# Walking the moving columns of TensorE products in interleaved order, in one decoder block

## The chip, the cores and the metric

The kernel runs on one core of one Trainium2 chip. The metric is the device time of one execution in microseconds (us), the median over the runs shown. Beside it stands one profiled execution, whose trace gives every instruction's start and duration.

## The reference

One layer of a decoder block over 512 tokens of width 1024, in float32. What matters here:

```
proj = rmsnorm(x) @ w_in                     # split into q_r, k_r, v_r, g_r, q_s, k_s, v_s, gates
ret  = silu(g_r) * GroupNorm(retention(q_r, k_r, v_r))     # v_r, g_r: 512 x 1024
y_r  = ret @ w_ret_out;   y_s = sliding_window_attention(q_s, k_s, v_s) @ w_swa_out
x    = x + rmsnorm((sigmoid(gate_r) * y_r + sigmoid(gate_s) * y_s) @ w_out)
u    = square(relu(rmsnorm(x) @ w_up))       # 512 x 4096
x    = x + rmsnorm(u @ w_down)               # the down projection: 4096 -> 1024
```

## The kernel before

**Arithmetic.** Every large product is done in three passes of a rounded float32 type (fp32r): an operand is split into a rounded part and a remainder (`parts`, `split`, lines 135 and 136: a cast on ScalarE, ACT in the profile, and a subtraction on VectorE, DVE), and `mm3` (lines 179 to 181) issues three matmuls into the same accumulator. A matmul has a stationary operand of 128 x 128, which a weight load (PEld) brings in, and a moving operand whose columns stream through, 256 or 512 of them; result column c lands in column c of a bank of the accumulator memory (PSUM).

**Seven products in place of eight.** The large products are split 2 x 2 into blocks and formed by a Strassen-Winograd scheme. Two of these products have weights as the moving operand and are the ones in question.

*The retention's values and gates* (`wide`, for `w_v` and then `w_g`). The weights, in blocks of 512 columns that the host lays out (`wide_blocks`), or sums of blocks added in flight by DMA, are split (`moving_parts`) and streamed. Seven products of 2 token tiles x 4 contraction tiles x 3 passes are 168 matmuls of 512 columns for each of the two weights. The accumulators are tiles named `wide`; ScalarE and VectorE bring them into `vg`. `wide` is a generator: the caller steps it between other work, some 55 to 106 us after the start for the values and 164 to 207 us for the gates.

*The down projection* (554 us to the end). Seven products `p1` to `p7` run over the same 512 columns; the left operands are blocks of `uc` (`left`), the moving ones blocks of `w_down`, or sums that DMAs accumulate into `tch[j]` and `rb[j]` (`right`). Each runs over four chunks j, and in each over 2 x 2 contraction tiles, 2 token tiles and 3 passes: 24 matmuls for a chunk, 96 for a product (`product2`). One tile of `w_down` goes through several products. The steps stand in an order written out by hand: `p1`, `p2` and `p5` in turn; then for each j `p6`, `p3` and the `p7` of the chunk before; then `p4`. Of `p4`, 72 matmuls have 512 columns; the last 16 x 3 are done in halves of 256 columns, in tiles named `p4c`. The profile leaves digits out of names, so `p1` to `p7` are all called `p` there.

Blocks of weights come in by DMAs that SyncE (SP) and GpSimd (POOL) issue. Between these products stand the sliding-window attention, the gates and the up projection (`wino`, 256 columns), `pblk`, `yr`, `ys` and `ps`.

Of the kernel before, what the change touches and what calls it, by code (L numbers as in the profile page):

```python
# [16 lines left out]
P = 128  # L17
# [21 lines left out]
C_QR, C_KR, C_VR, C_GR, C_QS, C_KS, C_GATE_R = (0, 512, 1024, 2048, 3072, 3584, 3840)  # L39
# [42 lines left out]
    return np.ascontiguousarray(t)  # L82


def wide_blocks(w):

    return np.ascontiguousarray(w.reshape(2, 4, P, 2, 512).transpose(3, 0, 2, 1, 4))


def f(ap):  # L90
# [4 lines left out]
def block_kernel(ctx, tc, x, xT, pre_mix, w_in, w_v, w_g, w_gate, w_ret, w_swa, w_out, sinks, post_mix,  # L95
                 pre_mlp, w_up, w_down, post_mlp, decay, chunk, dist, out):
    nc = tc.nc
    x, out = x[0], out[0]
    w_in, w_ret, w_swa, w_out = (w[0] for w in (w_in, w_ret, w_swa, w_out))
# [31 lines left out]
    last = {}  # L131
# [467 lines left out]
    def wide_sums(pool, w_, **kw):  # L599

        both = pool.tile([P, 2, 4, 512], F32, name="acc", **kw)
        sx, sy = both[:, 0], both[:, 1]
        nc.sync.dma_start(sx, w_[1, 0])
        nc.gpsimd.dma_start(sx, w_[1, 1], accum_op=ALU.add)
        nc.sync.dma_start(sy, w_[0, 0])
        return sx, sy

    def wide(w_, sx, sy, out):

        def c(i, half, tb):  # L610
            return out[:, 2 * half + tb, i * 512 : (i + 1) * 512]

        def product(ps, w, y, first=True):
            for tb in range(2):
                for k in range(4):
                    mm3(
                        ps[tb], tuple(o[:, k, tb * P : (tb + 1) * P] for o in hB[y]), w[k],
                        first and k == 0, k == 3, not first,
                    )

        def two():
            return [bank([P, 512], "wide") for _ in range(2)]

        chain = two()
        w = moving_parts(sy)
        nc.gpsimd.dma_start(sy, w_[1, 0], accum_op=ALU.add)
        ws1 = moving_parts(sx)
        nc.gpsimd.dma_start(sx, w_[0, 0], accum_op=ALU.add)
        yield
        product(chain, w, "11")  # L630
        for tb in range(2):
            nc.scalar.copy(c(0, 0, tb), chain[tb])
        yield
        p5 = two()
        product(p5, ws1, "t1")
        for tb in range(2):
            last["copy"] = nc.scalar.copy(c(1, 1, tb), p5[tb])
        yield
        p2 = two()
        product(p2, moving_parts(wide_load(w_, 0, 1)), "21")  # L640
        for tb in range(2):
            nc.vector.tensor_tensor(c(0, 0, tb), p2[tb], c(0, 0, tb), op=ALU.add)
        yield
        with tc.issue_after(last["copy"].ins):
            w = moving_parts(sx)
        nc.gpsimd.dma_start(sx, w_[0, 1], accum_op=ALU.add)
        product(chain, w, "t2", False)
        for tb in range(2):
            nc.scalar.copy(c(0, 1, tb), chain[tb])
            nc.vector.tensor_tensor(c(0, 1, tb), c(0, 1, tb), c(1, 1, tb), op=ALU.add)  # L650
        yield
        product(chain, moving_parts(sy), "t3", False)
        for tb in range(2):
            after = nc.scalar.copy(c(1, 0, tb), chain[tb])
            nc.vector.scalar_tensor_tensor(
                c(1, 1, tb), c(1, 0, tb), -1.0, c(1, 1, tb), op0=ALU.mult, op1=ALU.subtract
            )
        yield
        product(chain, moving_parts(wide_load(w_, 1, 1)), "t4", False)
        for tb in range(2):  # L660
            nc.scalar.mul(c(1, 0, tb), chain[tb], -1.0)
        yield
        p3 = two()
        with tc.issue_after(after.ins):
            w = moving_parts(sx)
        product(p3, w, "22")
        for tb in range(2):
            nc.vector.tensor_tensor(c(0, 1, tb), p3[tb], c(0, 1, tb), op=ALU.add)
        yield
# [14 lines left out]
    for g in range(SWA_KV):  # L684
        ps = bank([P, SEQ])
# [5 lines left out]
    sv = wide_sums(accpool, w_v, tag="acc")  # L691
# [18 lines left out]
    def ret_query(w):  # L710
# [5 lines left out]
    qT, qc = ret_query(wqk[0])  # L716
    kT = ret_block(wqk[1])
    vg = vpool.tile([P, NT, D_MODEL], F32, name="vg", tag="vg")
    steps = wide(w_v, *sv, vg)
    next(steps)  # L720
    hB = wino_tokens(
        None, *(tuple(quad(a, i, j) for a in hT) for i in range(2) for j in range(2)),
        [quad(xTs, i, j) for i in range(2) for j in range(2)], hsum,
    )
# [15 lines left out]
    for h in range(RET_HEADS):  # L740
        if 0 < h < RET_HEADS - 1:
            wqk = load_qk(h + 1)
        v = parts(vg[:, :, h * RET_DV : (h + 1) * RET_DV], [P, NT, RET_DV])
        if h == RET_HEADS - 1:
            vg = vpool.tile([P, NT, D_MODEL], F32, name="vg", tag="vg")
            steps = wide(w_g, *wide_sums(xypool, w_g), vg)
            next(steps)
        kd = ret_keys(kT, h)
        pt = ret_scores(qT, kT, h)
        q_now = qc  # L750
        if h + 1 < RET_HEADS:
            qT = ret_block(wqk[0])
        else:
            next(steps)
        if h == 0:
            probs_t = swa_transpose(probs)
        states = ret_states(kd, v, h)
        if h == 0:
            swa_values(3, probs_t)

            bctx.close()
            gctx = ExitStack()
            wx = wino_pool(gctx)
            pad(wx, 64)
            xyctx = ExitStack()
            xypool = xyctx.enter_context(tc.tile_pool(name="xypool", bufs=1))
        if h + 1 < RET_HEADS:
            kT = ret_block(wqk[1])
        else:
            next(steps)  # L770
        ret_values(q_now, pt, states, v, h)
        if h + 1 < RET_HEADS:
            qc = [rpool.tile([P, SEQ - P], F32R, name=f"qc{i}", bufs=1) for i in range(2)]
            split(qc[0], qc[1], qT[:, P:])
# [117 lines left out]
    a = wino_first(gate_weights(0))  # L892
    for bp in range(KD // 2):
        a = gate(2 * bp, a, lambda: gate_weights(2 * bp + 1))
        wr = gate(2 * bp + 1, a, lambda: ret_weights(bp))
        if bp < KD // 2 - 1:
            a = wino_first(gate_weights(2 * bp + 2))
# [66 lines left out]
    for half in range(2):  # L964
        zs = [[None, None], [None, None]]
        for n in range(2):
            for t in range(2):
                tt = 2 * half + t
                ps = bank([P, 512])
# [6 lines left out]
        with tc.high_priority(offset=CHAIN_AHEAD):  # L976
            for t in range(2):
# [4 lines left out]
                for n in range(2):  # L982
                    c = slice(n * 512, (n + 1) * 512)
# [139 lines left out]
    a = wino_first(up_weights(NH))  # L1123
    for fp in range(NH, 16):
        a = up_pair(fp, a)
# [13 lines left out]
    def left(j, q):  # L1139
        hi, lo = (ring.tile([P, 4, 256], F32R, name=f"left{i}") for i in range(2))  # L1140
        split(hi, lo, uc[j][:, q])
        return hi, lo

    def right(src):
        return [parts(src[:, 2 * i : 2 * i + 2], [P, 2, 512]) for i in range(2)]

    def product(ps, a, b, h, first, last, tb, c=slice(0, 512)):
        for i in (2 * h, 2 * h + 1):
            mm3(
                ps[tb], tuple(o[:, i, tb * P : (tb + 1) * P] for o in a),  # L1150
                tuple(o[:, i % 2, c] for o in b[h]), first and i == 0, last and i == 3,
            )

    def product2(ps, j, a, b):
        for h in range(2):
            for tb in range(2):
                product(ps, a, b, h, j == 0, j == 3, tb)

    def t_add(dst, k, c, j):
        nc.gpsimd.dma_start(dst, w_down[k, c, j], accum_op=ALU.add)  # L1160
# [24 lines left out]
    def step_p2(j):  # L1185
        with tc.issue_after(last["chain2"].ins), tc.high_priority(offset=LEFT_AHEAD if j == 0 else 0):
            a, b = left(j, 2), right(load_b(1, 0, j, 4))
        product2(p2, j, a, b)

    def step_p5(j):  # L1190
        a, b = left(j, 1), right(tch[j])
        if j < T2_DMA:
            t_add(tch[j], 1, 1, j)

        nc.vector.tensor_tensor(uc[j][:, 1], uc[j][:, 1], uc[j][:, 0], op=ALU.add)
        nc.vector.tensor_tensor(uc[j][:, 0], uc[j][:, 3], uc[j][:, 1], op=ALU.subtract)
        product2(p5, j, a, b)

    for step, j in ((step_p1, 0), (step_p2, 0), (step_p1, 1), (step_p5, 0), (step_p2, 1),
                    (step_p1, 2), (step_p5, 1), (step_p2, 2), (step_p1, 3), (step_p5, 2),  # L1200
# [42 lines left out]
    p6, p3 = banks2("p6"), banks2("p3")  # L1243
    p7 = None
    rb = {}

    def step_p6(j):
        if j >= T2_DMA:
            nc.vector.tensor_tensor(tch[j], tch[j], rb[j], op=ALU.add)
        a, b = left(j, 1), right(tch[j])  # L1250
        t_add(tch[j], 1, 0, j)

        nc.vector.tensor_tensor(uc[j][:, 1], uc[j][:, 2], uc[j][:, 1], op=ALU.subtract)
        product2(p6, j, a, b)

    def step_p3(j):
        a, b = left(j, 1), right(rb[j])
        t_add(rb[j], 0, 1, j)
        product2(p3, j, a, b)

    def step_p7(j):
        product2(p7, j, left(j, 0), right(rb[j]))

    for j in range(4):
        rb[j] = load_b(1, 1, j)
# [22 lines left out]
    for j in range(2):  # L1288
        a, b = left(j, 3), right(tch[j])
        for h in range(2):  # L1290
            for tb in range(2):
                product(p4, a, b, h, j == 0, j == 1 and tb == 1, tb)
        combine(j)
    ab = [(left(j, 3), right(tch[j])) for j in (2, 3)]
    for tb in range(2):
# [4 lines left out]
            residual(tb, factor(tb), ((0, outz[tb]), (512, p1c[tb])))  # L1300
    for j in (2, 3):
        for h in range(2):
            product(p4, *ab[j - 2], h, False, j == 3, 0)
    nc.vector.tensor_tensor(u3[0], p4[0], u3[0], op=ALU.subtract)
    squares(2, 1, u3[0])
    weigh(0, u3[0])
# [59 lines left out]
```

## Time and profile before

| | |
|---|---|
| runs | 721.85 and 724.63 us, median 723.24 us |
| profiled execution | span of 719.9 us from the first to the last instruction; no time of its own outside the span is given for it |
| TensorE (PE) | 708.3 us busy, 4438 matmuls and as many weight loads |
| VectorE, ScalarE, GpSimd | 535.8, 421.7 and 60.3 us busy |
| granted TensorE clock | 0.999 |
| HBM | 114.96 MB read, 163 GB/s over the span |

In the rows of the profile, "128*128 128x512" after a matmul's names are the stationary shape and the moving operand's partitions and columns. A matmul's own duration (390 ns for 512 columns, on the page) overlaps with the next matmul; what a matmul costs in a stream is the distance from its start to the next one's, and it is read from the timeline.

### The profile page before, as it was taken

Reading aid. Unit: us, or ns where it says so; the run is one execution under the profiler, and the core shown is the slowest. Engines: PE = TensorE matmul, PEld = TensorE weight load, DVE = VectorE, ACT = ScalarE, POOL = GpSimd, SP = SyncE. Lnnn points to the kernel's source line nnn. Section 1 sums busy time; section 2 is a strip of 40 time slices with the busy share of each in tenths; the row PEclk is TensorE's granted clock in tenths of the full one; section 3 lists DMA queues with packets and bytes.
Section 4 is the critical chain, followed back from the end, with each engine's and each line's share of the span. In section 5 each row is a group of like instructions: output and inputs, shape, how many; then the busy total and the mean of one; then the engine's idle time right before and its main releaser. Section 6 shows DMA issues by size and latency. Waiting matters only on the chain.

```text
span 719.9 us, 11248 instructions
## 1 busy us (share of the span) xinstructions
PE 708.3 (98%) x4438; PEld 628.8 (87%) x4438; DVE 535.8 (74%) x808; ACT 421.7 (59%) x712; POOL 60.3 (8%) x75
## 2 busy tenths in 40 slices
PE   8999999999999999999999999999999999999996
PEld 7877878888888989989888999999999888888885
DVE  5699986667885667566845876877776788977797
ACT  6667676345665526344643776666668666655571
POOL 0200000201100000000002100000000110010010
PEclk9999999999999999999999999999999999999999
DMA  9964424916444455461563618777753999698603
GB/s 318 330 179 84 108 72 129 282 46 132 101 142 120 107 162 147 125 197 59 198 271 117 159 47 234 201 202 193 204 153 118 305 278 238 151 208 194 118 0 117
DMA packets 43605, 117.79 MB, mean 164 GB/s; under 512 B 3488, under 2 KB 21024, under 8 KB 37408
## 3 DMA queue, kind: packets, MB, share of 16 engines
q1 hardware_dynamic: 36784, 80.76, 31.8%
q0 software_dynamic: 6480, 36.18, 27.3%
q8 instruction: 35, 0.57, 0.3%
q14 instruction: 18, 0.15, 0.1%
q10 hardware_dynamic: 288, 0.14, 0.1%
HBM read 114.96 MB, written 2.10 MB: 163 GB/s over the span
## 4 chain that ended last, share of the span: by engine, by line
PE 79%; DVE 8%; DMA 5%; ACT 4%; issue 2%; POOL 0%; POOLq 0%; DVEq 0%; SPq 0%; ACTq 0%
PE wino L179 9%; PE wino L180 9%; PE wino L181 9%; PE p L181 5%; PE p L180 5%; PE p L179 5%; DVE wlo L136 3%; PE wide L179 3%; PE wide L180 3%; PE wide L181 3%; DMA raw<-in_w_in 3%; PE ps L180 2%; PE ps L181 2%; PE yr L181 2%; PE yr L180 2%; PE yr L179 2%
## 5 line engine op out<-in xcount | busy, mean ns | idle before, releaser
L136 DVE TENSOR_TENSOR wlo<-raw,whi 128x1024 fp32r<-128x1024 f32 x81 | 98.6, 1223 | 42.4 <-ACT whi L135 42.2
L135 ACT CAST whi<-raw 128x1024 fp32r<-128x1024 f32 x81 | 84.8, 1052 | 40.4 <-DMA raw<-in_w_down 7.6
L181 PE MATMUL p<-whi,left 128*128 128x512 f32 x216 | 84.1, 390 | 0.2 <-DVE left L136 0.2
L180 PE MATMUL p<-wlo,left 128*128 128x512 f32 x216 | 84.2, 390 | 0.0
L179 PE MATMUL p<-whi,left 128*128 128x512 f32 x216 | 84.0, 390 | 0.1
L181 PEld LDWEIGHTS p<-whi,left 128*128 128x128 f32 x216 | 40.5, 188 | 9.3 <-DVE left L136 1.0
L180 PEld LDWEIGHTS p<-wlo,left 128*128 128x128 f32 x216 | 40.5, 188 | 8.9 <-DVE wlo L136 0.4
L179 PEld LDWEIGHTS p<-whi,left 128*128 128x128 f32 x216 | 40.5, 188 | 8.7 <-ACT left L135 0.5
L136 DVE TENSOR_TENSOR wlo<-tch,whi 128x1024 fp32r<-128x1024 f32 x32 | 38.6, 1220 | 6.9 <-ACT whi L135 6.9
L135 ACT CAST left<-uc 128x1024 fp32r<-128x1024 f32 x28 | 29.3, 1050 | 23.4 <-PE p L180 23.4
L135 ACT CAST p<-rs 128x1024 fp32r<-128x1024 f32 x21 | 22.1, 1051 | 35.5 <-DVE rs L230 35.4
L136 DVE TENSOR_TENSOR left<-uc,left 128x1024 fp32r<-128x1024 f32 x28 | 34.1, 1221 | 10.4 <-ACT left L135 10.4
L135 ACT CAST whi<-tch 128x1024 fp32r<-128x1024 f32 x32 | 33.2, 1050 | 11.3 <-PE p L181 6.8
L136 DVE TENSOR_TENSOR p<-rs,p 128x1024 fp32r<-128x1024 f32 x21 | 25.7, 1226 | 15.4 <-ACT p L135 15.4
L136 DVE TENSOR_TENSOR wlo<-rs,whi 128x1024 fp32r<-128x1024 f32 x21 | 25.7, 1224 | 12.1 <-ACT whi L135 9.4
L136 DVE TENSOR_TENSOR wlo<-acc,whi 128x1024 fp32r<-128x1024 f32 x20 | 24.1, 1217 | 6.5 <-ACT whi L135 6.5
L179 PE MATMUL wino<-h2s,p 128*128 128x256 f32 x104 | 28.7, 276 | 0.0
L180 PE MATMUL wino<-h2s,p 128*128 128x256 f32 x104 | 28.7, 276 | 0.0
L181 PE MATMUL wino<-h2s,p 128*128 128x256 f32 x104 | 28.7, 276 | 0.0
L179 PE MATMUL wino<-h2c,whi 128*128 128x256 f32 x104 | 28.7, 276 | 0.0
L180 PE MATMUL wino<-h2c,whi 128*128 128x256 f32 x104 | 28.7, 276 | 0.0
L181 PE MATMUL wino<-h2c,wlo 128*128 128x256 f32 x104 | 28.7, 276 | 0.0
(354 smaller groups left out, 2317.7 us busy)
## 6 DMA issues: line engine op xcount, KB each, us to landing
tch<-in_w_down POOLq DMA_DIRECT2D x12, 1024.0 KB, 9.5
raw<-in_w_down SPq DMA_DIRECT2D x7, 1024.0 KB, 7.6
rs<-in_w_up SPq DMA_DIRECT2D x13, 512.0 KB, 4.2
rs<-in_w_up POOLq DMA_DIRECT2D x13, 512.0 KB, 5.7
raw<-in_w_up SPq DMA_DIRECT2D x13, 512.0 KB, 5.1
raw<-in_w_in SPq DMA_DIRECT2D x8, 512.0 KB, 5.2
acc<-in_w_v POOLq DMA_DIRECT2D x4, 1024.0 KB, 7.9
rs<-in_w_gate SPq DMA_DIRECT2D x8, 512.0 KB, 3.9
```

The costliest lines, as they stand in the source:

```text
L135: last["hi"] = nc.scalar.copy(hi, src)
L136: last["split"] = nc.vector.tensor_tensor(lo, src, f(hi), op=ALU.subtract)
L179: nc.tensor.matmul(ps, ah, bh, start=first, stop=False, skip_group_check=more)
L180: nc.tensor.matmul(ps, ah, bl, start=False, stop=False, skip_group_check=more)
L181: nc.tensor.matmul(ps, al, bh, start=False, stop=last, skip_group_check=more)
```

## The change

A pair (n, e) describes a walk. The 512 columns are seen as n blocks of equal size, and each block as runs of e columns. The walk takes the first run of every block, then the second run of every block, and so on. With (2, 4): columns 0 to 3, 256 to 259, 4 to 7, 260 to 263, ... Before, all columns are taken from 0 to 511.

| product | walk (n, e) | run, bytes | matmuls of 512 columns |
|---|---|---|---|
| values (`w_v`) | (2, 4) | 16 | 168 |
| gates (`w_g`) | (2, 16) | 64 | 168 |
| `p1` | none | | 96 |
| `p2` | (2, 4) | 16 | 96 |
| `p5` | (2, 16) | 64 | 96 |
| `p6` | (2, 2) | 8 | 96 |
| `p3` | (2, 32) | 128 | 96 |
| `p7` | (4, 8) | 32 | 96 |
| `p4` | (2, 64) | 256 | 72 |

In the down projection, the moving operand and the accumulator are both walked in this order, so every result column lands where it did. In `wide`, the host permutes the columns of each block of 512 beforehand; the walk undoes this, so the moving operand is read in the interleaved order while the accumulator is written from column 0 to 511. The halves of `p4c` keep the plain order. No instruction, DMA or wait is added or taken away in the source.

```
+ORDER_V, ORDER_G = (2, 4), (2, 16)
-def wide_blocks(w):
-    return np.ascontiguousarray(w.reshape(2, 4, P, 2, 512).transpose(3, 0, 2, 1, 4))
+def wide_blocks(w, order):
+    n, e = order
+    t = w.reshape(2, 4, P, 2, 512).transpose(3, 0, 2, 1, 4)
+    t = t.reshape(2, 2, P, 4, 512 // (n * e), n, e).transpose(0, 1, 2, 3, 5, 4, 6)
+    return np.ascontiguousarray(t.reshape(2, 2, P, 4, 512))
...
-    def wide(w_, sx, sy, out):
+    def wide(w_, sx, sy, out, order):
+        n, e = order
+        def streamed(ap):
+            return ap.rearrange("p (n q e) -> p q n e", n=n, e=e)
...
                     mm3(
-                        ps[tb], tuple(o[:, k, tb * P : (tb + 1) * P] for o in hB[y]), w[k],
+                        ps[tb].rearrange("p (q n e) -> p q n e", n=n, e=e),
+                        tuple(o[:, k, tb * P : (tb + 1) * P] for o in hB[y]),
+                        tuple(streamed(o) for o in w[k]),
                         first and k == 0, k == 3, not first,
                     )
...
-    def product(ps, a, b, h, first, last, tb, c=slice(0, 512)):
+    def streamed(ap, order):
+        if not order:
+            return ap
+        n, e = order
+        return ap.rearrange("p (n q e) -> p q n e", n=n, e=e)
+
+    def product(ps, a, b, h, first, last, tb, c=slice(0, 512), order=None):
         for i in (2 * h, 2 * h + 1):
             mm3(
-                ps[tb], tuple(o[:, i, tb * P : (tb + 1) * P] for o in a),
-                tuple(o[:, i % 2, c] for o in b[h]), first and i == 0, last and i == 3,
+                streamed(ps[tb], order), tuple(o[:, i, tb * P : (tb + 1) * P] for o in a),
+                tuple(streamed(o[:, i % 2, c], order) for o in b[h]), first and i == 0, last and i == 3,
             )
...
-        product2(p2, j, a, b)
+        product2(p2, j, a, b, (2, 4))
...
-        product2(p5, j, a, b)
+        product2(p5, j, a, b, (2, 16))
-        product2(p6, j, a, b)
+        product2(p6, j, a, b, (2, 2))
-        product2(p3, j, a, b)
+        product2(p3, j, a, b, (2, 32))
-        product2(p7, j, left(j, 0), right(rb[j]))
+        product2(p7, j, left(j, 0), right(rb[j]), (4, 8))
...
-                product(p4, a, b, h, j == 0, j == 1 and tb == 1, tb)
+                product(p4, a, b, h, j == 0, j == 1 and tb == 1, tb, order=(2, 64))
```

More of the change, by code (lines that the diff above doesn't have):

```diff
@@ L718, in block_kernel @@
     vg = vpool.tile([P, NT, D_MODEL], F32, name="vg", tag="vg")
-    steps = wide(w_v, *sv, vg)
+    steps = wide(w_v, *sv, vg, ORDER_V)
     next(steps)
@@ L745, in block_kernel @@
             vg = vpool.tile([P, NT, D_MODEL], F32, name="vg", tag="vg")
-            steps = wide(w_g, *wide_sums(xypool, w_g), vg)
+            steps = wide(w_g, *wide_sums(xypool, w_g), vg, ORDER_G)
             next(steps)
@@ L1145, in right, with product2 @@
         return [parts(src[:, 2 * i : 2 * i + 2], [P, 2, 512]) for i in range(2)]
-    def product(ps, a, b, h, first, last, tb, c=slice(0, 512)):
+    def streamed(ap, order):
[4 more added lines that the diff above has]
+    def product(ps, a, b, h, first, last, tb, c=slice(0, 512), order=None):
         for i in (2 * h, 2 * h + 1):
             mm3(
-                ps[tb], tuple(o[:, i, tb * P : (tb + 1) * P] for o in a),
-                tuple(o[:, i % 2, c] for o in b[h]), first and i == 0, last and i == 3,
+                streamed(ps[tb], order), tuple(o[:, i, tb * P : (tb + 1) * P] for o in a),
+                tuple(streamed(o[:, i % 2, c], order) for o in b[h]), first and i == 0, last and i == 3,
             )
-    def product2(ps, j, a, b):
+    def product2(ps, j, a, b, order=None):
         for h in range(2):
             for tb in range(2):
-                product(ps, a, b, h, j == 0, j == 3, tb)
+                product(ps, a, b, h, j == 0, j == 3, tb, order=order)
     def t_add(dst, k, c, j):
@@ L1302, in block_kernel @@
         for h in range(2):
-            product(p4, *ab[j - 2], h, False, j == 3, 0)
+            product(p4, *ab[j - 2], h, False, j == 3, 0, order=(2, 64))
     nc.vector.tensor_tensor(u3[0], p4[0], u3[0], op=ALU.subtract)
@@ L1348 @@
         pre_mix_norm=np.asarray(inputs["pre_mix_norm"]).reshape(KD, P).T,
-        w_v=wide_blocks(w_in[0, :, C_VR:C_GR]),
-        w_g=wide_blocks(w_in[0, :, C_GR:C_QS]),
+        w_v=wide_blocks(w_in[0, :, C_VR:C_GR], ORDER_V),
+        w_g=wide_blocks(w_in[0, :, C_GR:C_QS], ORDER_G),
         w_gate=pair_blocks(w_in[0, :, C_GATE_R:]),
```

## The prediction

> **What bounds the kernel now.** I read the page first, then the waits of TensorE, then the groups by shape, then the timeline for the distance between matmuls.
>
> ```profile
> span 719.9 us, 11248 instructions
> PE 708.3 (98%) x4438; PEld 628.8 (87%) x4438; DVE 535.8 (74%) x808; ACT 421.7 (59%) x712; POOL 60.3 (8%) x75
> PE 79%; DVE 8%; DMA 5%; ACT 4%; issue 2%; POOL 0%; POOLq 0%; DVEq 0%; SPq 0%; ACTq 0%
> ```
>
> TensorE is busy for 98% of the span, and 79% of the chain that ended last is its own work. The waits say the same; these are all that TensorE has:
>
> ```profile
> PE warm L336 <- POOL ident masks.py:199: 1.4, 1, 1.4
> PE ptok L179 <- ACT wkv L135: 1.3, 1, 1.3
> PE swa_s L430 <- ACT vg L637: 0.6, 1, 0.6
> PE pblk L181 <- DVE wlo L136: 0.5, 1, 0.5
> PE wino L179 <- ACT sgs L283: 0.2, 1, 0.2
> PE wide L179 <- ACT vg L654: 0.2, 1, 0.2
> PE tin L1040 <- ACT uc L1031: 0.2, 1, 0.2
> PE p L181 <- DVE left L136: 0.2, 1, 0.2
> ```
>
> They sum to 4.6 us in 720. So the time is the sum of the distances between matmuls, and a nanosecond on one of them reaches the end. The groups that the change touches, by count:
>
> ```profile
> L179 PE MATMUL p<-whi,left 128*128 128x512 f32 x216 | 84.0, 390 | 0.1
> L180 PE MATMUL p<-wlo,left 128*128 128x512 f32 x216 | 84.2, 390 | 0.0
> L181 PE MATMUL p<-whi,left 128*128 128x512 f32 x216 | 84.1, 390 | 0.2 <-DVE left L136 0.2
> L179 PE MATMUL wide<-whi,hsum 128*128 128x512 f32 x64 | 25.4, 397 | 0.2 <-ACT vg L654 0.2
> L179 PE MATMUL wide<-whi,hT 128*128 128x512 f32 x48 | 19.2, 399 | 0.0
> ```
>
> Three lines of 216 are the 648 matmuls of `p`; without the 96 of `p1`, which keeps its order, 552 change. `wide` has 64 + 48 on each of three lines, 336, and all change. Together 888 of 512 columns. Their 390 ns is passage, not cost; the cost is the distance between starts:
>
> ```profile
> 562.02 0.39 PE L179 MATMUL p<-whi,left 128*128 128x512 f32 x1
> ...
> 565.88 0.39 PE L181 MATMUL p<-whi,left 128*128 128x512 f32 x1
> 124.80 0.39 PE L180 MATMUL pblk<-hT,whi 128*128 128x512 f32 x1
> ...
> 127.37 0.40 PE L179 MATMUL pblk<-hT,whi 128*128 128x512 f32 x1
> 239.99 0.28 PE L179 MATMUL wino<-hsum,whi 128*128 128x256 f32 x1
> ...
> 242.48 0.28 PE L180 MATMUL wino<-hT,whi 128*128 128x256 f32 x1
> 269.93 0.28 PE L181 MATMUL wino<-hsum,wlo 128*128 128x256 f32 x1
> ...
> 271.93 0.28 PE L180 MATMUL wino<-hsum,p 128*128 128x256 f32 x1
> 392.94 1.91 PE L1040 MATMUL tin<-ident,zg 128*128 128x128 f32 x16
> ```
>
> From the first to the last of 18 `p` matmuls are 17 steps: 3.86 / 17 = 227.1 ns. Twelve of `pblk`, same shape, take 2.57 / 11 = 233.6 ns each. Of the 256-column ones, 23 take 2.49 / 22 = 113.2 ns and, 30 us later, 18 take 2.00 / 17 = 117.6 ns. Two things follow. Cost goes with the columns (227.1 is twice 113.2; 0.443 ns a column), with nothing left over for an instruction. And the same instruction on other tiles is up to 6.5 ns dearer (227.1 to 233.6), so how the columns are fetched does show.
>
> **The change part by part.** *What stays.* The counts of matmuls, weight loads, casts and DMAs are those of before, and no step is moved past another on any queue. The host's permutation of `w_v` and `w_g` leaves the blocks their shape, so their DMAs stay; sums and splits go element by element and do not care about column order. Accumulators end with the same columns in the same places, so what reads them stays. I cost all this at nothing, and no cover is needed for it.
>
> *What the walk costs on the 888 matmuls.* No row of this trace has a matmul that reads or writes in pieces, so I bound it by the nearest rows. Above: the slowest stream is that of the transposes (the x16 row above; one lasts 273 ns by the next row). (1.91 - 0.273) / 15 = 109 ns for 128 columns is 0.852 ns a column, about twice 0.443.
>
> ```profile
> L1040 PE MATMUL tin<-ident,zg 128*128 128x128 f32 x32 | 4.0, 273 | 0.2 <-ACT uc L1031 0.2
> L135 ACT CAST whi<-raw 128x1024 fp32r<-128x1024 f32 x81 | 84.8, 1052 | 40.4 <-DMA raw<-in_w_down 7.6
> L135 ACT CAST left<-uc 128x1024 fp32r<-128x1024 f32 x28 | 29.3, 1050 | 23.4 <-PE p L180 23.4
> ```
>
> A matmul of 512 columns at that rate costs 512 x 0.852 = 436 ns, 209 ns more than now; over 888 that would be 186 us. Below: if a column of a transpose takes two passes through the array, one pass is 0.426 ns at most, and a stream without loss would take 218 ns in place of 227.1: 9.0 ns saved on each, 8.0 us in all. Between these ends the nearest row is ScalarE's: 12 of the 81 casts from `raw` read eight runs of 128 columns out of 256 (lines that slice `raw[:, :, b * P : (b + 1) * P]`), and the group's mean is 1052 ns against 1050 for the plain reads of `left<-uc`. Twelve dearer ones in 81 can then hide 2 x 81 / 12 = 14 ns at most, under 2 ns a run. It is another engine and the runs are longer than any of the walk's, but it is the only row in which a walk in pieces is priced, and it prices it at next to nothing. So I take **nothing** for the walk, with both ends kept for the rivals.
>
> *Placement.* Within "nothing" the 6.5 ns between `p` and `pblk` stay open, as a walk also alters which part of memory is read at which moment: 888 x 6.5 ns = 5.8 us either way.
>
> *What is late next.* A slower stream gives the other engines more room. A faster one would run into them in the down projection:
>
> ```profile
> 554.00:631.00 77.00, 76.84 (x360) 63.81 (x358) 64.55 (x62) 48.66 (x56) 8.20 (x10) 1.00 0.89 239
> 631.00:704.00 73.00, 72.93 (x322) 60.12 (x321) 60.19 (x64) 43.00 (x49) 7.79 (x9) 1.00 0.61 126
> ```
>
> The columns are length, busy time of TensorE, weight loads, VectorE, ScalarE and GpSimd, clock, DMA share and GB/s. VectorE has 12 us spare in each stretch, so the 5 us that the down projection could gain would stay covered, except in the first stretch, where the DMA engines are at 0.89.
>
> *The sum.* The span is 719.9 us and the median of the runs shown 723.24, 3.3 us more, which I leave as lying around the span. 723.2 + 0 = **723.2 us**.
>
> *A page against it.* The trace has no row of a matmul that writes its accumulator in pieces. The Trainium skill, "PSUM — Partial Sum Buffer", section "Specifications (TRN2)", says that accumulator lines are 8 bytes and that any output that isn't contiguous slows matmuls significantly. By that, the 552 of `p` would be dear and the 336 of `wide`, written straight, would not; it is the third rival, priced there from rows. The Trainium skill, "SBUF — State Buffer", section "Specifications (TRN2)", asks for two hits on a 16-byte line for full rate; counted in columns every walk here fulfils that, `p6` with its pairs only just, and the sum would stay at nothing.
>
> **The rivals.** *First, slower: short runs starve the stream.* If the fetch of moving columns brings in some fixed piece for each jump, a run that is too short leaves the array without columns. The place is `p6`, whose runs are two columns, 8 bytes. Price: the transposes' rate, 96 x 209 ns = 20.1 us, **743 us**. It decides from the point where the 8 bytes of a run last less than the fetch of the next piece. For it: the 6.5 ns between two places suggest that the fetch has little slack. Against it: nothing but ScalarE's row. If 16 bytes are too short as well, `p2` and the values (96 + 168 = 264) add 264 x 209 ns = 55.2 us: 723.2 + 20.1 + 55.2 = 798.5 us.
>
> *Second, slower by less: a small loss at each piece.* Suppose the 9.0 ns that a matmul of 512 columns may lose now comes at 32 borders of 16 columns, 0.28 ns each; the 16 is my assumption, as the trace shows only the total. Then runs of 16 and more are free; runs of 8 have 32 more borders (9 ns x 96 = 0.9 us), runs of 4 have 96 more (27 ns x 264 = 7.1 us), pairs 224 more (63 ns x 96 = 6.0 us). Sum 14.0 us, **737 us**. With pairs at the first rival's price: 723.2 + 20.1 + 7.1 + 0.9 = 751.3 us, the worst mixture that I take as usual.
>
> *Third, slower: the accumulator.* If writing in pieces halves the rate whatever the run, 552 x 209 ns = 115.4 us, **839 us**. It would show in `p2` to `p7` alike, 436 ns between starts, with `wide` untouched.
>
> *Fourth, faster: the walk hides the present loss.* 888 x 9.0 ns = 8.0 us, **715 us**. For it: the loss goes with the columns, so something in reading them in a row makes it. Against it: none of the stretches above shows less than 227.1 ns.
>
> A walk that the program folds back into the plain order would give 723.2 as well; two blocks 1024 bytes apart can't be described by one step, so I give this no share of its own.
>
> **How the numbers follow.** Forecast (nothing but placement, 717 to 729) 0.44; first rival 0.22, and 0.05 for its form with 16 bytes; second 0.14; third 0.08; fourth 0.07. The range leaves out the third rival and the 16-byte form, 0.13, and a little of the edges: from 713 (the fourth, less 2 us for the spread of the two runs) to 752 (the mixture). A measurement of this kernel tells about 2%, 14.5 us, from no change: below 708.8 is faster, above 737.7 slower. Slower: 0.22 + 0.05 + 0.08 + half of the second, whose sum lies on the bound, 0.07, make 0.42. Faster: only the edge of the fourth, as all of the loss in the trace is 1.1%; 0.02. Within: 0.56.
>
> **What would show it.** `p1` is the control: its 227 ns between starts must stay. Under the forecast every other product shows 220 to 234. The first rival shows 436 in `p6` alone, the second a ladder (`p6` 290, `p2` and values 254, `p7` 236, the rest 227), the third 436 in `p2` to `p7` with values and gates at 227 to 233, the fourth 218. Values against `p2`, and gates against `p5`, have the same walk with a straight and with a walked accumulator, so a difference between them belongs to the accumulator. I am wrong if any product but `p1` moves by more than 7 ns, or if the order of instructions on TensorE differs, since the distances then no longer add up as here.

## The result, and the profile after

The first comparison gave 746.21 us (746.17 and 746.25) against 723.24 us, a ratio of 1.0287 with a 95% interval of 1.0224 to 1.0351. Timed again with more runs of both (below), it is 1.0246 (1.0206 to 1.0287). The change makes the kernel slower by about 18 us. Ratios leave out runs that lie over 1.5% above the fastest of their kernel (one, in the last experiment).

The page of the changed kernel has TensorE at 99% of a longer span; the other engines' busy times are those of before (DVE 536.3, ACT 423.6 us).

```profile
span 744.5 us, 11250 instructions
PE 735.0 (99%) x4438; PEld 638.5 (86%) x4438; DVE 536.3 (72%) x808; ACT 423.6 (57%) x712; POOL 59.5 (8%) x75
```

The timeline of the changed kernel answers product by product. Each pair below is the first and the last matmul of one uninterrupted stretch: values, gates, 256-column matmuls of the up projection, then p5, p2, p1, p6, p3, p7 (one chunk each, 24 matmuls) and p4 (72). (Lines 185 to 187 here are lines 179 to 181 of the kernel before.)

```profile
79.44 0.51 PE L185 MATMUL wide<-whi,hsum 128*128 128x512 f32 x1
...
85.33 0.43 PE L187 MATMUL wide<-whi,hsum 128*128 128x512 f32 x1
174.11 0.40 PE L185 MATMUL wide<-whi,hsum 128*128 128x512 f32 x1
...
179.63 0.40 PE L187 MATMUL wide<-whi,hsum 128*128 128x512 f32 x1
554.75 0.28 PE L186 MATMUL wino<-h2d,p 128*128 128x256 f32 x1
...
558.99 0.28 PE L186 MATMUL wino<-h2s,p 128*128 128x256 f32 x1
604.11 0.40 PE L185 MATMUL p<-whi,left 128*128 128x512 f32 x1
...
609.63 0.40 PE L187 MATMUL p<-whi,left 128*128 128x512 f32 x1
609.87 0.41 PE L185 MATMUL p<-whi,left 128*128 128x512 f32 x1
...
615.63 0.41 PE L187 MATMUL p<-whi,left 128*128 128x512 f32 x1
615.87 0.40 PE L185 MATMUL p<-whi,left 128*128 128x512 f32 x1
...
621.13 0.39 PE L187 MATMUL p<-whi,left 128*128 128x512 f32 x1
671.87 0.51 PE L185 MATMUL p<-whi,left 128*128 128x512 f32 x1
...
679.53 0.50 PE L187 MATMUL p<-whi,left 128*128 128x512 f32 x1
679.87 0.40 PE L185 MATMUL p<-whi,left 128*128 128x512 f32 x1
...
685.32 0.40 PE L187 MATMUL p<-whi,left 128*128 128x512 f32 x1
685.55 0.40 PE L185 MATMUL p<-whi,left 128*128 128x512 f32 x1
...
690.87 0.39 PE L187 MATMUL p<-whi,left 128*128 128x512 f32 x1
715.88 0.39 PE L185 MATMUL p<-whi,left 128*128 128x512 f32 x1
...
732.00 0.39 PE L187 MATMUL p<-whi,left 128*128 128x512 f32 x1
```

A stretch of 24 has 23 steps (p4: 71). In the trace of before, undisturbed stretches of `p` stand at 226.7 ns. The cost is what all starts of a product spread over more than in that trace, waits included:

| product | walk, run | distance in the rows above | cost, us |
|---|---|---|---|
| p1 (control) | plain | 5.26 / 23 = 228.7 ns | 0.2 |
| p4 | (2, 64), 256 B | 16.12 / 71 = 227.0 | -0.3 (a wait of before is gone) |
| p7 | (4, 8), 32 B | 5.32 / 23 = 231.3 | 0.4 |
| p3 | (2, 32), 128 B | 5.45 / 23 = 237.0 | 1.0 |
| p5 | (2, 16), 64 B | 5.52 / 23 = 240.0 | 1.3 |
| p2 | (2, 4), 16 B | 5.76 / 23 = 250.4 | 2.3 |
| p6 | (2, 2), 8 B | 7.66 / 23 = 333.0 (325 to 333 by chunk) | 9.9 |
| gates | (2, 16), 64 B | 5.52 / 23 = 240.0 | 1.6 (mean 230.9 to 240.5) |
| values | (2, 4), 16 B | 5.89 / 23 = 256.1 | 3.6 (mean 235.2 to 256.6) |

The stretch of values holds one step of 348 ns, which the same place before has too (339). Without such long steps (over 262 ns) the values go from 229.4 to 251.1 ns and the gates from 229.1 to 240.0. That is where p2 (250.4) and p5 (240.0) stand, which have the same walks but walk the accumulator as well: the first sign that the accumulator's order costs nothing. And p1, with no walk of its own, stands 2 ns above its 226.7 of before; why a plain product among walked ones is a little dearer stays open.

From trace to trace the starts of `p` spread over 14.8 us more and those of `wide` over 5.2 us more: 20.0 of the span's 24.6. Most of the rest has nothing walked in it: the 37 `wino` matmuls above stand 4.24 / 36 = 117.8 ns apart where the same stage had 113 before. `wino` and `up` (256 columns too) take 5.9 us more, the first projection `ptok` 2.0 more, and pieces of attention, `pblk` and the end 3.2 less. The experiments had to tell whether that, too, belongs to the change.

### The profile page after: what moved, and what is told of

It is laid out like the page before. It is cut to its first block, busy times and chain, and to the rows that moved or that the text cites. A ratio compares the mean times of both kernels' runs of the same rounds, so it can differ in the third digit from the quotient of the medians.

```text
span 744.5 us, 11250 instructions
## 1 busy us (share of the span) xinstructions
PE 735.0 (99%) x4438; PEld 638.5 (86%) x4438; DVE 536.3 (72%) x808; ACT 423.6 (57%) x712; POOL 59.5 (8%) x75
## 4 chain that ended last, share of the span: by engine, by line
PE 94%; DMA 2%; DVE 2%; ACT 1%; issue 1%; POOL 0%; POOLq 0%; DVEq 0%; SPq 0%; ACTq 0%
PE wino L185 9%; PE wino L187 9%; PE wino L186 9%; PE p L186 7%; PE p L185 7%; PE p L187 7%; PE wide L185 4%; PE wide L187 4%; PE wide L186 4%; PE pblk L185 3%; PE pblk L187 3%; PE pblk L186 3%; PE ps L185 2%; PE ps L187 2%; PE yr L187 2%; PE yr L185 2%
## 5 line engine op out<-in xcount | busy, mean ns | idle before, releaser
L186 PE MATMUL p<-wlo,left 128*128 128x512 f32 x216 | 89.6, 415 | 0.2 <-DVE wlo L142 0.2
L187 PE MATMUL p<-whi,left 128*128 128x512 f32 x216 | 89.4, 415 | 0.0
L185 PE MATMUL p<-whi,left 128*128 128x512 f32 x216 | 89.3, 414 | 0.0
L141 ACT CAST whi<-tch 128x1024 fp32r<-128x1024 f32 x32 | 33.7, 1062 | 16.8 <-PE p L187 11.5
L185 PE MATMUL wino<-h2s,p 128*128 128x256 f32 x104 | 29.2, 281 | 0.0
L186 PE MATMUL wino<-h2s,p 128*128 128x256 f32 x104 | 29.2, 281 | 0.0
L187 PE MATMUL wino<-h2s,p 128*128 128x256 f32 x104 | 29.2, 281 | 0.0
L185 PE MATMUL wino<-h2s,whi 128*128 128x256 f32 x104 | 29.2, 281 | 0.0
```

What stands on the lines that cost most here:

```text
L141: last["hi"] = nc.scalar.copy(hi, src)
L185: nc.tensor.matmul(ps, ah, bh, start=first, stop=False, skip_group_check=more)
L186: nc.tensor.matmul(ps, ah, bl, start=False, stop=False, skip_group_check=more)
L187: nc.tensor.matmul(ps, al, bh, start=False, stop=last, skip_group_check=more)
```

## The experiments

**The kernel before, once more.** 

> The kernel before once more, unchanged, for a second trace. In the first trace the 256-column matmuls of the gates, the up projection and the first projection stood 113 ns apart in long stretches and 118 ns in others (1764 of wino at 115.0 on average), in the trace of the changed kernel nearly all at 118 (117.8). Theory 1 (the 113 and 118 are states that a run falls into, nothing to do with the walk): the stretches lie elsewhere here, the mean of wino differs from 115.0 by 1 ns or more, and the span with it by some us. Rival (the changed kernel's walks or its two more waits on TensorE cause the 118): wino stays at 115.0 with the same stretches, span within 1 us of 719.9.

721.49 us, span 719.7, and the same stretches: `wino` at 114.9 ns on average, fast from 411 us to 560 us as in the first trace. By this run alone the rival, that the change causes the 118 ns, stood.

**The accumulator alone.** The walk goes to the other side: the host stores the columns in walked order, so the moving operand is read straight.

```
+ORDER_V, ORDER_G = (2, 2), (8, 2)
+    t = t.reshape(2, 2, P, 4, n, 512 // (n * e), e).transpose(0, 1, 2, 3, 5, 4, 6)
-                        ps[tb], tuple(o[:, k, tb * P : (tb + 1) * P] for o in hB[y]), w[k],
+                        ps[tb].rearrange("p (n q e) -> p q n e", n=n, e=e),
+                        tuple(o[:, k, tb * P : (tb + 1) * P] for o in hB[y]), w[k],
```

> The kernel before, with the accumulator of values and gates alone walked: the host permutes the columns so that the moving operand is read straight, and the result columns are put in place by the walk of the accumulator, (2, 2) for the values and (8, 2) for the gates. Theory 1 (the cost is in reading the moving operand): both stay where they were, 226 to 232 ns between starts, ratio 1.00. Rival (the cost is in writing the accumulator in pieces): the values rise to about 333 ns as p6 with its pairs did, 168 x 104 = 17 us, and the gates as far.

727.19 against 727.05 us, ratio 0.9994 (0.9961 to 1.0027). The timeline of this kernel, one stretch of values and one of gates:

```profile
78.58 0.50 PE L185 MATMUL wide<-whi,hsum 128*128 128x512 f32 x1
...
83.96 0.40 PE L187 MATMUL wide<-whi,hsum 128*128 128x512 f32 x1
171.28 0.40 PE L185 MATMUL wide<-whi,hsum 128*128 128x512 f32 x1
...
176.54 0.39 PE L187 MATMUL wide<-whi,hsum 128*128 128x512 f32 x1
```

5.38 / 23 = 233.9 and 5.26 / 23 = 228.7 ns; the mean of all 336 is 232.9 against 233.1 before. Writing the accumulator in runs of 8 bytes costs nothing here; the cost is in reading the moving operand. This trace also has something for the other question: its span is 726.2 us, and it is 6.4 us longer than that of before in `wino` (5.2), `up` (0.9) and `ptok` (2.4) with 2.2 less elsewhere, while the down projection has no walk at all and wide is unchanged. So the 118 ns come without any walk of the moving operand.

**One walk undone.** `product2(p6, j, a, b, (2, 2))` back to `product2(p6, j, a, b)`.

> The changed kernel with p6 alone put back to the plain order. Theory 1 (each product pays for its own walk, and the costs add): p6 falls from 333 to 227 ns, 96 x 106 = 10.1 us, so 736 us, and all other products keep their distance (p2 250, p5 240, p3 238, p7 231, p4 227). Rival (something common to the walks, such as a wait or a lag that builds up, costs the time): less than 5 us come back, and the other products move too. If the 256-column matmuls fall into their faster state in this run, up to 8 us more go.

735.65 us (729.45 to 737.10), ratio 1.0124 (1.0083 to 1.0164). The timeline: one chunk of p6, then one of p3.

```profile
661.56 0.40 PE L185 MATMUL p<-whi,left 128*128 128x512 f32 x1
...
666.81 0.39 PE L187 MATMUL p<-whi,left 128*128 128x512 f32 x1
667.04 0.40 PE L185 MATMUL p<-whi,left 128*128 128x512 f32 x1
...
672.48 0.40 PE L187 MATMUL p<-whi,left 128*128 128x512 f32 x1
```

p6 is at 5.25 / 23 = 228.3 ns, its neighbour p3 stays at 5.44 / 23 = 236.5. The down projection falls from 14.8 to 5.9 us above before. The costs add, product by product, and half of the whole is p6. As p1 does in the changed kernel, the plain p6 stands about 2 ns above the 226.7 of before. This run's 256-column matmuls were at 113 ns in the up projection though seven of the eight walked products were still walked, so these walks don't hold them at 118.

**The walk by itself.** A kernel of its own: a stationary and a moving operand lie ready, 36 matmuls of 512 columns for each walk; only VectorE works beside TensorE, adding up each finished accumulator.

> Not the block: 36 matmuls in a row for each of 28 walks, stationary and moving operands lying ready, no other engine at work; the output is a meaningless sum. Moving operand alone walked, accumulator straight: theory 1a (a loss per run of columns, the prediction's second rival) gives a distance that falls with the run alone, whatever the number of blocks: (2,2) 333, (2,4) 251, (2,8), (4,8), (8,8), (16,8), (32,8) all about 231, 16 and more 227. Rival 1b (which part of memory follows which decides): equal runs differ with the distance of the blocks, (2,8) is not (4,8), and (2,16) stays dearer than (4,8) as in the changed kernel (240 against 231). Accumulator alone walked: 227 by theory 1. Both walked: as the moving operand alone. Plain order from another first column (8, 16, 24): 227 by 1a, up to 236 by 1b. A walk under 227 would be a way to a faster kernel.

The groups of this kernel by shape. Busy time less one passage, over 35 steps, is the distance; the rounding of the busy time leaves 1.5 ns.

```profile
L84 PE MATMUL ba<-mov,sta 128*128 128x512 f32 x36 | 12.4, 512 | 0.0
L84 PE MATMUL ma<-mov,sta 128*128 128x512 f32 x36 | 12.2, 502 | 0.0
...
L84 PE MATMUL mm<-mov,sta 128*128 128x512 f32 x36 | 9.4, 421 | 0.0
L84 PE MATMUL mb<-mov,sta 128*128 128x512 f32 x36 | 9.2, 416 | 0.0
...
L84 PE MATMUL mc<-mov,sta 128*128 128x512 f32 x36 | 8.9, 406 | 0.0
...
L84 PE MATMUL plainh<-mov,sta 128*128 128x512 f32 x36 | 8.6, 395 | 0.0
...
L84 PE MATMUL mi<-mov,sta 128*128 128x512 f32 x36 | 8.5, 394 | 0.0
...
L84 PE MATMUL mo<-mov,sta 128*128 128x512 f32 x36 | 8.4, 392 | 0.0
...
L84 PE MATMUL last<-mov,sta 128*128 128x512 f32 x36 | 8.4, 390 | 0.0
...
L84 PE MATMUL ab<-mov,sta 128*128 128x512 f32 x36 | 8.3, 389 | 0.0
...
L84 PE MATMUL mp<-mov,sta 128*128 128x512 f32 x36 | 8.2, 384 | 0.0
```

`ma`, (2, 2), takes (12.2 - 0.502) / 35 = 334 ns and `mb`, (2, 4), 251: the block's numbers to within the rounding, so nothing else of the block is needed to explain their size. `ab`, the accumulator alone in (8, 2), is at 226. `ba`, both walked in pairs as in p6, is at 340, somewhat above p6's 325 to 333. The plain order, `last`, is at 227.5 by its starts; from another first column (8, 16 or 24 further) it takes 233.4, 229.1 and 233.7 (`plainh` is the first of these). So the place of the moving operand alone moves the plain order by up to 6 ns, as much as lay between `p` and `pblk` before. From the starts themselves, in ns:

| run | 2 blocks | 4 | 8 | 16 | 32 | 64 |
|---|---|---|---|---|---|---|
| 16 B (e = 4) | 250.3 | 267.8 | 277.9 | 246.3 | 223.5 | 231.2 |
| 32 B (e = 8) | 243.4 | 231.6 | 256.3 | 230.3 | 232.3 | |
| 64 B (e = 16) | 240.0 | 231.8 | 239.7 | 239.9 | | |
| 128 B (e = 32) | 236.8 | 233.6 | 236.6 | | | |

(The 8 x 64 B, 16 x 64 B and 8 x 128 B cells are from the second such kernel below.) Each cell is one stretch of 36. Theory 1a falls: with runs of 32 bytes (`mc`, `mi`, `mm`, `mo`) the distance is 243, 232, 256 and 230, depending on how far apart the blocks lie. And one walk, `mp`, (32, 4), is under the plain order. What sets these distances beyond that, no run isolates.

**Both again, in many runs.**

> The changed kernel once more, timed beside the kernel before in many runs of both. In the runs so far the kernel before falls into two groups, about 721 and about 727 us, and the traces of both groups differ in the distance of the 256-column matmuls alone (113 or 118 ns). Theory (the walks cost 14.8 us in the down projection and 5.2 us in values and gates, and the two groups are there with any walk): the changed kernel has two groups as well, 19 to 20 us above the two of before, 740 and 746 us, ratio 1.026 to 1.028; the first two runs of before both lay in the faster group and the two of the changed kernel in the slower. Rival (the walks push the 256-column matmuls to 118 ns for good): all runs at 746 us.

744.62 us (739.70 to 746.58, 6 runs) against 727.68 (721.79 to 728.91, 17 runs). The changed kernel falls into two groups as before does, 739.7 and 741.9, and 744.4 to 746.6. This time its trace, of span 737.9 us, lies in the lower one. Its timeline, at the same place in the up projection:

```profile
554.80 0.28 PE L186 MATMUL wino<-h2c,whi 128*128 128x256 f32 x1
...
558.99 0.28 PE L187 MATMUL wino<-h2s,wlo 128*128 128x256 f32 x1
```

38 matmuls, 4.19 / 37 = 113.2 ns, in the same program that had 117.8. So the 113 and the 118 are not of the program. Against the first trace of before this one is 18.0 us longer: `p` 14.5, `wide` 5.2, and 1.7 less in the rest, of which 1.2 is in pieces of attention (`swa_s` and `pso`). As `swa_s` is 1.0 shorter in the accumulator-only trace too, where `wide` isn't slower, the walk isn't needed for most of that.

**More walks, shifted operands, 256 columns.**

> Not the block: 36 matmuls in a row for each case, as in the first such run; the output is a meaningless sum. More walks of 512 columns, (32, 4) with the first column of moving or stationary operand shifted by 32 or 64 bytes, and 256-column matmuls in the plain order (seven stretches) and walked. Theory 1 (the pace depends on which part of memory follows which in the moving operand alone): (32, 4) stays at 222 to 226 wherever the operands begin, and (16, 4) on 256 columns gives 110 to 113. Rival (moving and stationary reads meet in the memory): a shift of 64 bytes in one of the two moves (32, 4) and the plain order by 3 ns or more, and shifting both puts it back. Pairs with many blocks, (64, 2) and (128, 2): 333 if each run of 8 bytes costs, near 227 if runs whose 16-byte line was just read are cheap. The stretches of plain 256 columns all at 113 or all at 118 if the state is fixed for a run, mixed if a pause can change it.

Groups of this kernel by shape (`me` is (64, 2), `ma` (4, 2), `plains` the plain order with the stationary operand 64 bytes further, `na` (32, 4), `hc`, `hi` and `hf` the plain order on 256 columns):

```profile
L92 PE MATMUL me<-mov,sta 128*128 128x512 f32 x36 | 16.8, 651 | 0.0
...
L92 PE MATMUL ma<-mov,sta 128*128 128x512 f32 x36 | 16.2, 635 | 0.0
...
L92 PE MATMUL plains<-mov,sta 128*128 128x512 f32 x36 | 8.6, 395 | 0.0
...
L92 PE MATMUL plain<-mov,sta 128*128 128x512 f32 x36 | 8.3, 389 | 0.0
...
L92 PE MATMUL na<-mov,sta 128*128 128x512 f32 x36 | 8.2, 385 | 0.0
...
L92 PE MATMUL hi<-mov,sta 128*128 128x256 f32 x36 | 4.4, 280 | 0.0
...
L92 PE MATMUL hc<-mov,sta 128*128 128x256 f32 x36 | 4.4, 279 | 0.0
...
L92 PE MATMUL hf<-mov,sta 128*128 128x256 f32 x36 | 4.2, 276 | 0.0
```

Pairs over more than two blocks are far dearer than p6: `me` (16.8 - 0.651) / 35 = 461 and `ma` 445 ns; over 4 to 128 blocks they take 431 to 487, about half rate. Moving the stationary operand by 64 bytes puts the plain order from 226.7 to 233.4 ns by the starts, so the place of the stationary operand matters as well, against theory 1 and as the rival had it; that the two reads meet in the memory is the rival's reading, and no run shows where. In (32, 4) shifts of one operand or of both move the distance between 224.1 and 227.5 ns, less for one alone than the 3 ns of the rival, and (2, 16) stays at 239.9. Shifting both for (32, 4) didn't put it back (227.5), against the rival. The same plain 256 columns stood 118 ns apart in four stretches (`ha`, `hc`, `hi`, `hl`) and 113 in one (`hf`), within one run. No pause stands between the stretches: `hf` begins about 118 ns after the last matmul of the stretch before it, which was walked. So the pace can change in the middle of a stream. (16, 4) on 256 columns gave 116, not the 110 to 113 of theory 1.

**The better walk everywhere.** In the kernel before:

```
+    def walked(ap):
+        if len(ap.shape) != 2 or ap.shape[1] != 512:
+            return ap
+        return ap.rearrange("p (n q e) -> p q n e", n=32, e=4)
...
         (ah, al), (bh, bl) = a, b
+        ps, bh, bl = walked(ps), walked(bh), walked(bl)
```

> The kernel before with one walk, (32, 4), in every matmul of 512 columns, moving operand and accumulator (1752 of them): 32 blocks of 64 bytes, of each the first 16 bytes, then of each the second, and so on. By itself this walk gave 223.5 ns between starts where the plain order gave 226.7. Theory (the moving operand's order sets the pace here too): the 512-column products go to 222 to 227 ns, 1752 x 3.2 = 5.6 us come off, more where pblk and wide now take 229 to 236; ratio about 0.99. Rival (in the block other engines read the same memory and break the pattern): 227 or more, ratio 1.00 or above.

719.68 us (716.61 to 727.81, 12 runs) against 727.68, ratio 0.9909 (0.9875 to 0.9943): about 1% faster than the kernel before. The timeline: 48 matmuls of `yr`, and 144 of `ps`.

```profile
310.65 0.39 PE L186 MATMUL yr<-retT,whi 128*128 128x512 f32 x1
...
321.18 0.39 PE L188 MATMUL yr<-retT,wlo 128*128 128x512 f32 x1
357.79 0.38 PE L187 MATMUL ps<-wo,mhi 128*128 128x512 f32 x1
...
390.18 0.38 PE L186 MATMUL ps<-wo,mhi 128*128 128x512 f32 x1
```

`yr` is at 10.53 / 47 = 224.0 ns, as by itself; `ps` at 32.39 / 143 = 226.5, no better than plain. From trace to trace the 512-column products gain 2.6 (`pblk`), 1.0 (`wide`), 0.8 (`p`), 0.6 (`yr`) and 0.2 us (`ys`) and lose 0.8 (`ps`, in a wait on VectorE): 4.4 of the 5.6 us expected. Of `pblk`'s 2.6, 1.1 came in other traces without any walk of it. This trace as a whole, of span 722.3 us, is 2.4 us longer than that of before, as its up projection stood at 118 ns (`wino` 3.7 us more). Group against group the runs lie about 4 us apart: the lower ones (split at 721 and 724 us) 718.0 against 722.3 us on average, the upper ones 724.1 against 727.9. The ratio's 0.9% is more, 6.6 us, because fewer of these runs fell into the upper group; whether that comes from the walk, the runs do not show.

## Why the prediction was wrong

*What bounds the kernel:* right. 20.0 us of longer distances came out as 18 us of time; the rest are small gains in pieces that nobody walked. The first comparison, 23 us, was too large by chance: it set one run of before from the lower of its two groups and one from between them (721.85 and 724.63) against two runs of the changed kernel from the upper one.

*The step that failed* is "I take nothing" for the walk on the 888 matmuls. It rested on ScalarE's casts, whose runs are 512 bytes long, and their nearness was one of form only: another engine, and runs at least twice as long as any of the walk's. At the run nearest to it, p4's 256 bytes, the row was a good guide (227.0 ns). At 128 bytes and below it was not: 0.4 to 9.9 us a product, 20.0 in all, against 5.8 us allowed for placement. The prediction's own `pblk` row, 6.5 ns dearer on other tiles, was the better neighbour: it hinted that reading has little slack, as the plain order from other first columns later showed (229.1 to 233.7 ns against 227.5). It should have moved the sum, not only its margin.

*Where the columns are written:* right that nothing there need cost, and the third rival (839 us) is excluded by the accumulator-only run and by p4 and p7, which walk the accumulator at 227 and 231 ns. The Trainium skill, "PSUM — Partial Sum Buffer", section "Specifications (TRN2)", has any output that isn't contiguous slow a matmul significantly; runs of 8 bytes gave 232.9 against 233.1 ns, so for these the measurement differs from the page.

*The first rival* had the place right, p6, and the price at twice what came: 333 ns, not 436, 9.9 us and not 20.1. The half rate it assumed exists, but in pairs over four and more blocks (431 to 487 ns). The Trainium skill, "SBUF — State Buffer", section "Specifications (TRN2)", asks for two hits on a 16-byte line; a pair is two columns of one line, and 333 to 487 ns show that two columns are not enough for this stream. The same row of the Trainium skill has each cross to a new line pay a penalty, which the prediction left out; pairs change line twice as often as the plain order, but what one crossing costs no run isolates.

*The second rival* had the ladder nearly right for short runs (predicted 254, 236 and 290 for p2, p7 and p6; measured 250, 231 and 333) and the sum too low (14.0 against 20.0 us). Its reason is wrong: runs of 64 and 128 bytes, free by it, cost 240 and 237 ns, and equal runs differ with the distance of the blocks, by up to 54 ns (16 bytes, 223.5 to 277.9).

*The fourth* was right that a walk can hide part of the present loss; none of this change's walks does.

*"The counts are those of before":* nearly. TensorE's stream has two waits more, one on VectorE and one on its own earlier matmuls (11250 instructions for 11248), with the matmuls in the same order; its waits in the profile sum to 3.2 us against 4.6, so they cost nothing that shows.

*The reference point:* 723.24 us was the median of two runs. In 36 later ones before was under 724 us 10 times and between 726 and 730 the other 26. Of this spread of up to 8.6 us, over 1%, the 5 to 6 between the groups were in the trace as two distances of one instruction, 113.2 and 117.6 ns; the prediction named both and gave them no cost.

## What to carry to other kernels

When TensorE streams without a pause, price a change of access pattern per column read: one ns on 888 matmuls is 0.9 us. Interleave the accumulator if it helps (in pairs of columns or longer), but keep fp32r moving operands straight unless the very walk has been timed by itself; 36 matmuls per case in a small kernel gave most of the block's numbers to within a nanosecond (p6's pairs came out 2 to 4% lower in the block, and (32, 4) held its 223 to 224 ns in part of the products alone). And look at several runs of the kernel before, and at a stage that the change doesn't touch, ahead of crediting a change with the last one per cent.

## What the runs showed of the hardware that was not expected

- Reading order alone moves a 512-column fp32r matmul between 223.5 and 487 ns with the same columns, shapes and counts. It isn't monotone in the run's length: 32 blocks with runs of 16 bytes (223.5) beat the plain order (226.7), 8 blocks with such runs take 277.9. The rule behind it stays open.
- Where the stationary operand lies shifts the plain order from 226.7 to 233.4 ns (64 bytes); where the moving operand begins does the same (229.1 to 233.7 ns from other columns).
- The same 256-column matmuls stand 113 or 118 ns apart for hundreds of matmuls on end. Which of the two differs between runs of one program and can change within a stream that never pauses. It goes with the two groups of run times, 5 to 6 us apart: in all seven traces of the block, those from lower groups have the up projection at 113 and those from upper groups at 118. What sets it stays open.
